# Keys turned by rows in layer 0, and exponents packed without holes in layer 1

## The chip, the cores and the metric

The kernel runs on one core of a Trainium2 chip. The metric is the device time of one execution in microseconds (us). The engines are TensorE (PE), VectorE (DVE), ScalarE (ACT), GpSimd (POOL) and SyncE (SP), which here only issues DMAs. Each engine works off its own list of instructions in order; semaphores make one wait for another.

## The reference

The reference is a decoder trunk of two layers for one sequence of 1024 tokens and width 1024, in float32. Layer 0 is gated linear attention, layer 1 sparse attention; after each mixer come a residual sum with LayerNorm and a gated per-layer embedding.

```
# layer 0: four heads, key width 256, value width 512
q_t = q * dk**-0.5 * exp(G);  k_t = k * exp(-G);  k_s = k * exp(G_last - G)
A = where(tril, q_t @ k_t.T, 0);  o = A @ v + q_t @ S
S = S * decay + k_s.T @ v                     # state, chunk after chunk
o = o * rsqrt(mean(o*o) + eps) * gn_g;  y = (o * silu(z)) @ w_out
# layer 1: sixteen heads of width 128, one shared k and v
idx = top 256 of the indexer's scores of each query
o = softmax(q @ k[idx].T * scale) @ v[idx];  y = (o * silu(z)) @ w_out
```

## The kernel before

The work is cut into two halves of 512 tokens, and both layers run half by half: layer 0 of half 0, layer 0 of half 1, layer 1 of half 0, layer 1 of half 1. An operand of a float32 matmul is split into a high and a low part in the rounded type fp32r (ACT makes the high part, DVE the low one by a subtraction); a product is then three matmuls, high by high, high by low and low by high. All projections are such matmuls of 128x512 into PSUM tiles named `pb` or `U`. Their weights (`wst`) come from DRAM and are split into `whi` and `wlo` in half 0; the parts are stored as `whs` and `wls`, and half 1 loads them from there.

The program is written in one stream by Python. A `Flow` object keeps an estimated clock of PE and a heap of steps with due times: `after(dt, f)` makes a step due dt after now, `req` puts a step back until its inputs have been emitted, `ripe(t)` until the estimated clock has reached t. The order on every engine is thus fixed when the program is built, by estimates; on the chip only semaphores wait.

**Layer 0, one head of one half.** `v_phase` makes the values of four chunks of 128 tokens, each in a loop over four 128-wide parts (t) and the two halves of the weights (kk). `qk_phase` makes the queries and keys; DVE writes the scaled keys as `m` (`ev_k`). Then four chunks go through `s1` to `s4`. `s1` computes A transposed into `tr` and, where a state follows, turns the chunk's keys with two matmuls against `ident`; `kh` and `kl` are their high and low parts. `s2` updates the state through `U`, the next step forms o, and `s4` passes on: for most heads o is turned in squares of 32 by DVE and through DRAM (`od`, `uf`), for the last head's later chunks by four transposes on PE (`oT`). The result, gated, is `u`, the operand of the output matmuls. `R` holds the states, `sc0` is scratch.

**Layer 1, `attend`.** Half 1 sees 512 past keys and its own 512; half 0 only its own. For each head and each block t of 128 queries, PE computes scores `S`; DVE adds the mask and takes the minimum (`P`, `mx`, L1592); ACT writes the exponents to `sq` with their sum (L1599). `sq` holds for each t all key blocks j up to its own; blocks above the diagonal are holes that stay zero. DVE turns `sq` in squares of 32 (L1605). SP stores it (`sqd`, L1618), four DMAs for each group i of 512 keys, and loads it back turned as `PT` (L1628), one DMA for each group. ACT and DVE split `PT` into `ph` (L1645) and the low part, which stays in `PT` (L1643), and PE multiplies with the values `vT` into `o` (three matmuls for each key block). `sq` is one tile, so a head's exponents wait until the stores of the head before have landed. The loop over heads runs in slots: while head h is multiplied with the values, the scores of head h + 1 are made, and two or three units of projections (L329, `slots`) fill PE. In half 1 slots 0 to 3 have two units, from slot 4 on three.

The lines with names such as L58 (a matmul) and L411 (a low part) are helpers.

Of the kernel before, what the change touches and what calls it, by code (L numbers as in the profile page):

```python
# [23 lines left out]
HT = 512  # L24
NK = 8
GH = 4
# [251 lines left out]
def trunk_kernel(ctx, tc, x_tok, x_T, p_T, pos, freq, g_q, g_k, g_v, g_z, g_a, g_a2, g_ba, g_gn, g_o,  # L278
# [329 lines left out]
    def qk_phase(u, X):  # L608
# [4 lines left out]
        def ev_q(d):  # L613
# [9 lines left out]
            return f  # L623

        def ev_k(d):
            def f(ps):
                dve.tensor_mul(u["k"][:, d], ps, u["k"][:, d])
            return f

# [16 lines left out]
    def core_steps(u):  # L646
# [31 lines left out]
        def s1(c):  # L678
            def f():
                cs = slice(c * 128, c * 128 + 128)  # L680
                if c == 0 and half:
                    make_S(0)
                tr = pp.tile([128, 4, 128], F32, tag="tr", name="tr")
                for d in range(2):
                    mm(tr[:, 0], k[:, d, cs], q[:, d, cs], d == 0, d == 1)
                if makes_state(c):
                    for d in range(2):
                        fl.transpose(tr[:, 1 + d], k[:, d, cs], ident)
                Af = Afs[c % 2]
                Ah = lp.tile([128, 128], F32R, tag="Ah", name="Ah", bufs=2)  # L690
# [4 lines left out]
                def a():  # L695
                    dve.copy_predicated(Af, cmask, tr[:, 0])
                    if makes_state(c):
                        act.activation(kh, tr[:, 1:3], AF.Copy)

                def b():  # L700
                    if makes_state(c):
                        lo_part(kl, tr[:, 1:3], kh)
                        st["kt", c] = kh, kl
# [97 lines left out]
        def s4(c):  # L801
            def f():
# [752 lines left out]
    def attend(st, h, half, ap, sq):  # L1555
# [7 lines left out]
        G, nb = len(groups), half + 1  # L1563
        by_key = sq.rearrange("p (b j t r) -> p t j b r", b=4, t=4, r=32)
        squares = sq.rearrange("p (b j t r) -> p t b j r", b=4, t=4, r=32)

# [4 lines left out]
        def A(t):  # L1571
            def f():
# [9 lines left out]
                if t == 0:  # L1582
                    st["sm", h] = cp.tile([128, 4], F32, tag=("ss", "rs")[h % 2], name="sm", bufs=2)
                    st["mx", h] = cp.tile([128, 3, 8], F32, tag="mid", name="mx", bufs=2)
                sm, mx = st["sm", h], st["mx", h][:, 0, t:t + 1]
                lim = 3.0e38
# [9 lines left out]
                def exp():  # L1596
                    fl.req(st["x"] == nb * h)
                    to, rows = by_key[:, t, :n // 128], P.rearrange("p (j b r) -> p j b r", b=4, r=32)
                    act.activation(to, rows, AF.Exp, scale=-1.0, bias=mx, accum_out=sm[:, t:t + 1])  # L1599
                    st["P", h, t] = True  # L1600
                    after(0.4 + n / 1000.0, turned)

                def turned():
                    x = squares[:, t, :, :n // 128]
                    dve.transpose(x, x)  # L1605
                    st["D", h, t] = True
# [3 lines left out]
        def store(i):  # L1610

            def f():
                get(*(("D", h, t) for t in range(4)))
                fl.req(st["x"] == nb * h + i)
                dt = st["dram", h, i] = dp.tile([4, 32, 4, HT], F32, tag=f"sq{i}", name="sqd", bufs=2)
                sq4 = sq.rearrange("p (b i c) -> p i b c", b=4, i=nb)
                for a in range(4):
                    nc.sync.dma_start(dt[:, :, a].rearrange("b p c -> p b c"), sq4[32 * a:32 * a + 32, i])  # L1618
                st["x"] += 1
            return f  # L1620

        def load(i):

            def f():
                dt, _ = get(("dram", h, i), ("dram", h, nb - 1))
                fl.req(st["pv"] >= (h * G - (0 if i else G - 4) if half else (h - 1) * G))
                PT = ap.tile([128, 4, HT], F32R, tag=f"PT{i}", name="PT", bufs=2 - half)
                nc.sync.dma_start(PT.bitcast(F32), dt.rearrange("b p a c -> (b p) a c"))  # L1628
# [3 lines left out]
        def parts(g):  # L1632
            def f():
# [3 lines left out]
                st["sp"] += 1  # L1637
                lo = PT.rearrange("p a (j c) -> p j a c", c=128)[:, j % 4, :, 32 * t0:]
                ph = ap.tile([128, HT], F32R, tag="ph", name="ph", bufs=3)
                hi = ph[:, :HT - 128 * t0].rearrange("p (a c) -> p a c", a=4)  # L1640

                def second():
# [7 lines left out]
        def inverse():  # L1650
            get(("P", h, 3))
            fl.req(st["x"] > nb * h)
            row = st["row", h] = dp.tile([4, 128], F32, tag="row", name="row", bufs=2)
            if in_turn:
                dve.reciprocal(st["sm", h], st["sm", h])
# [30 lines left out]
        def pv(g):  # L1686
            first, last = g == 0, g == len(groups) - 1

            def f():
# [8 lines left out]
                if last:  # L1698
                    PT, = get(("PT", h, half))
                    whole = PT.bitcast(F32).rearrange("p a (j c) -> p j a c", c=128)[:, 3, :, 96:]  # L1700
                    mm(o3[:, :, 96:], vT[0][:, base + 3].bitcast(F32), whole, False, False)
                for i, (l, r) in enumerate(((vT[0], ph), (vT[1], ph), (vT[0], pl))):
                    mm(o3[:, :, 32 * t0:], l[:, j], r, first and i == 0, last and i == 2)
                if g == len(groups) - 2:
# [3 lines left out]
                if last:  # L1708
# [10 lines left out]
                    def done():  # L1719
# [96 lines left out]
    for half in range(NH):  # L1816
# [6 lines left out]
        fl.run(*(unit(u) for u in first_units))  # L1823
        sq = ap.tile([128, (4 * half + 4) * HT], F32, name="sq")
        pool.memset(sq, 0.0)
        st["x"] = st["sp"] = st["pv"] = st["out"] = 0
# [3 lines left out]
        for h, units in enumerate(plan, -1):  # L1830
# [5 lines left out]
            if h >= 0:  # L1836
# [16 lines left out]
            if h < 15:  # L1853
# [117 lines left out]
```

## Time and profile before

| | us |
|---|---|
| median of three runs | 1934.23 (1932.59 to 1935.04) |
| the profiled execution | 1935.94 |
| its span | 1934.2 |
| PE busy | 1914.7 (99%) |
| DVE busy | 1495.4 (77%) |
| ACT busy | 1002.4 (52%) |
| POOL busy | 153.0 (8%) |

The profile is one execution; the span runs from the first instruction to the last. PE's busy time counts overlapping ends of pipelined matmuls, so the time between starts tells what a matmul costs. Hardware DMA queues were busy for 72.1% of sixteen engines' span. In the timeline a row gives start, duration, engine, line, operation, output and inputs, shapes, and in brackets how long the engine had been idle and who ended it. `SPq` is SP issuing a DMA; its time is that of the issue, not of the transfer.

### The profile page before, as it was taken

Reading aid. Unit: us, or ns where it says so; the run is one execution under the profiler, and the core shown is the slowest. Engines: PE = TensorE matmul, PEld = TensorE weight load, DVE = VectorE, ACT = ScalarE, POOL = GpSimd, SP = SyncE. Lnnn points to the kernel's source line nnn. Section 1 sums busy time; section 2 is a strip of 40 time slices with the busy share of each in tenths; the row PEclk is TensorE's granted clock in tenths of the full one; section 3 lists DMA queues with packets and bytes.
Section 4 is the critical chain, followed back from the end, with each engine's and each line's share of the span. In section 5 each row is a group of like instructions: output and inputs, shape, how many; then the busy total and the mean of one; then the engine's idle time right before and its main releaser. Section 6 shows DMA issues by size and latency. Waiting matters only on the chain.

```text
span 1934.2 us, 26875 instructions
## 1 busy us (share of the span) xinstructions
PE 1914.7 (99%) x8826; PEld 1590.6 (82%) x8826; DVE 1495.4 (77%) x3081; ACT 1002.4 (52%) x1896; POOL 153.0 (8%) x301
## 2 busy tenths in 40 slices
PE   9999999999999999999999999999999999999999
PEld 7888888888888888888888888888888778888887
DVE  5777666696778888878858987778798887777873
ACT  5564636445564646464535676756443443434432
POOL 0000000010010101010101001221001010000000
PEclk9999999999999999999999999999999999999999
DMA  4567766768667767677688588987877898888874
GB/s 156 207 218 230 225 220 215 225 207 274 223 221 262 244 224 247 222 242 228 211 287 302 169 294 288 318 293 283 305 247 283 324 305 302 299 303 289 290 285 142
DMA packets 200764, 488.91 MB, mean 253 GB/s; under 512 B 26504, under 2 KB 42928, under 8 KB 194480
## 3 DMA queue, kind: packets, MB, share of 16 engines
q1 hardware_dynamic: 193200, 474.55, 72.1%
q0 software_dynamic: 7424, 12.64, 2.0%
q8 instruction: 69, 1.13, 0.2%
q14 instruction: 71, 0.58, 0.1%
HBM read 343.18 MB, written 143.92 MB: 252 GB/s over the span
## 4 chain that ended last, share of the span: by engine, by line
PE 88%; DVE 5%; ACT 3%; DMA 2%; issue 1%; SPq 0%; DVEq 0%; ACTq 0%
PE pb L58 67%; PE o L58 8%; PE U L58 6%; PE S L58 5%; DMA PT<-sqd 1%; PE tr L58 1%; DVE sq L1605 1%; DVE PT L1643 0%; DMA wst<-in_g_v 0%; DVE sc L1141 0%; PE xt L62 0%; DVE wlo L191 0%; PE ix L58 0%; SPq L1618 0%; PE S L62 0%
## 5 line engine op out<-in xcount | busy, mean ns | idle before, releaser
L58 PE MATMUL pb<-x,whi 128*128 128x512 f32 x2272 | 704.2, 391 | 0.8 <-DVE x L411 0.7
L58 PEld LDWEIGHTS pb<-x,whi 128*128 128x128 f32 x2272 | 419.5, 188 | 80.0 <-DVE x L411 1.9
L58 PE MATMUL pb<-x,wlo 128*128 128x512 f32 x1136 | 442.6, 390 | 0.0
L58 PE MATMUL pb<-whi,u 128*128 128x512 f32 x1024 | 339.5, 392 | 1.5 <-ACT u L419 0.8
L58 PEld LDWEIGHTS pb<-x,wlo 128*128 128x128 f32 x1136 | 213.2, 188 | 45.8 <-DVE wlo L191 0.4
L58 PEld LDWEIGHTS pb<-whi,u 128*128 128x128 f32 x1024 | 192.2, 188 | 41.3 <-ACT u L419 1.2
L58 PE MATMUL pb<-wlo,u 128*128 128x512 f32 x512 | 199.6, 390 | 0.0
L191 DVE TENSOR_TENSOR wlo<-wst,whi 128x512 fp32r<-128x512 f32 x232 | 154.5, 683 | 35.1 <-ACT whi L189 34.9
L189 ACT ACTIVATE whi<-wst 128x512 fp32r<-128x512 f32 x232 | 136.4, 622 | 73.9 <-DMA wst<-in_g_k 28.8
L1599 ACT ACTIVATE sq<-P,mx 128x128 f32<-128x128 f32 (+7 forms) x128 | 98.8, 772 | 87.6 <-DVE mx L1592 58.0
L58 PE MATMUL S<-kT,q 128*128 128x512 f32 (+2 forms) x576 | 123.6, 343 | 1.7 <-DVE q L411 1.2
L1645 ACT ACTIVATE ph<-PT 128x512 fp32r<-128x512 f32 (+2 forms) x160 | 86.2, 558 | 63.0 <-PE o L58 43.4
L58 PEld LDWEIGHTS S<-kT,q 128*128 128x128 f32 x576 | 100.4, 188 | 20.5 <-DVE mx L1592 2.1
L58 PEld LDWEIGHTS pb<-wlo,u 128*128 128x128 f32 x512 | 96.2, 188 | 18.2
L1643 DVE TENSOR_TENSOR PT<-PT,ph 128x512 fp32r<-128x512 f32 (+2 forms) x160 | 92.6, 592 | 21.4 <-ACT ph L1645 21.2
L1207 ACT ACTIVATE tk<-sc,tki 128x768 f16<-128x768 f32 (+2 forms) x90 | 92.9, 1033 | 25.4 <-DVE tki L1216 21.6
L1605 DVE STREAM_TRANSPOSE sq<-sq 128x128 f32<-128x128 f32 (+7 forms) x128 | 97.7, 768 | 2.0 <-ACT sq L1599 2.0
L237 DVE TENSOR_TENSOR pst<-pst,phi 128x512 fp32r<-128x512 f32 x130 | 88.7, 682 | 7.4 <-ACT phi L233 7.4
L753 ACT ACTIVATE junk<-o 128x512 bf16<-128x512 f32 x32 | 19.1, 597 | 139.7 <-DVE ot L748 116.6
L58 PE MATMUL o<-ph,vT 128*128 128x512 f32 (+2 forms) x320 | 90.8, 365 | 0.0
L58 PE MATMUL pb<-whi,x 128*128 128x512 f32 x256 | 85.3, 392 | 0.0
L58 PE MATMUL U<-whi,x 128*128 128x512 f32 x256 | 84.6, 389 | 0.0
(330 smaller groups left out, 3400.4 us busy)
## 6 DMA issues: line engine op xcount, KB each, us to landing
whi<-whs SPq DMA_DIRECT2D x128, 512.0 KB, 6.1
wlo<-wls SPq DMA_DIRECT2D x128, 512.0 KB, 6.7
sqd<-sq SPq DMA_DIRECT2D x192, 256.0 KB, 4.4
PT<-sqd SPq DMA_DIRECT2D x48, 1024.0 KB, 7.7
whs<-phi SPq DMA_DIRECT2D x130, 256.0 KB, 4.1
wls<-pst SPq DMA_DIRECT2D x130, 256.0 KB, 4.1
wst<-in_g_z SPq DMA_DIRECT2D x32, 512.0 KB, 4.7
wst<-in_g_o SPq DMA_DIRECT2D x32, 512.0 KB, 5.1
```

The costliest lines, as they stand in the source:

```text
L58: self.pe.matmul(out, lhsT, rhs, start=start, stop=stop)
L189: self.nc.scalar.activation(hi[:, c], st[:, c], AF.Copy, scale=1.0 if gain is None else gain)
L191: self.nc.vector.tensor_sub(lo[:, c], st[:, c], hi[:, c].bitcast(F32))
L237: self.nc.vector.tensor_sub(st, st.bitcast(F32), hi.bitcast(F32))
L753: act.activation(junk, ps, AF.Square, accum_out=u["ss"][:, c:c + 1])
L1207: act.activation(junk()[:, :n], scs[j], AF.Sign, bias=cand[:, j:j + 1].bitcast(F32), accum_out=cnt[:, j:j + 1])
L1599: act.activation(to, rows, AF.Exp, scale=-1.0, bias=mx, accum_out=sm[:, t:t + 1])
L1605: dve.transpose(x, x)
L1643: dve.tensor_sub(lo, lo.bitcast(F32), hi.bitcast(F32))
L1645: chain((0, lambda: act.activation(hi, lo.bitcast(F32), AF.Copy)), (0.8, second))
```

## The change

1. In `v_phase` the order of the matmuls, first half of the weights before the second, holds for the first three chunks of the first head instead of the first alone.
2. In half 0 of layer 0 the keys of chunks 2 and 3 (heads 0 and 3) or 1, 2 and 3 (heads 1 and 2) are turned by DVE in squares of 32 (`kq`), written to DRAM by POOL (`kd`) in eight DMAs a head and read back by one into `R` of the next head or `sc0`. `kh` and `kl` are made from there, and those chunks issue no transposes on PE.
3. For the last head `s4` is ripe 2.6 instead of 1.1 after o.
4. In layer 1 the ten unmasked cells (t, j) of a head's own exponents are packed in 320 columns for each of four rows b instead of 512. A block's past and own exponents are written by instructions of their own, with sums that DVE adds up afterwards. The memsets of `sq` go. Stores and loads of the own group become 320 columns wide. In half 1 the own `PT` gets two buffers, and its load stands ahead of the past one's.

```
-            if c == h == 0:
+            if c < 3 and h == u["half"] == 0:
                 order.sort(key=lambda x: x[1])
...
+    def turned_k(u):
+        return () if u["half"] else (2, 3) if u["h"] in (0, 3) else (1, 2, 3)
+
+    def turn_k(u, kd, d):
+        h, cs = u["h"], turned_k(u)
+        n = 32 * len(cs)
+        kq = lp.tile([128, HT], F32, tag=f"S{'hl'[d]}0", name="kq")
+        dve.transpose(kq[:, :4 * n].rearrange("p (m c i) -> p c m i", m=4, i=32), u["k"][:, d, 128 * cs[0]:])
+
+        def out():
+            for a in range(4):
+                pool.dma_start(kd[:, :, a, d].rearrange("m r x -> r m x"),
+                               kq[32 * a:32 * a + 32, :4 * n].rearrange("p (m x) -> p m x", m=4))
+            if d:
+                after(4.0, back_k)
+
+        def back_k():
+            raw = (R[h + 1].rearrange("p d t -> p (d t)") if h < GH - 1 else sc0)[:, :8 * n]
+            pool.dma_start(raw, kd.rearrange("m r a d x -> (m r) (a d x)"))
+            u["kt"] = raw.rearrange("p (a d c i) -> p c d a i", a=4, d=2, i=32)
+        after(1.0, out)
...
+                by_rows = c in turned_k(u)
+                fl.req(not by_rows or "kt" in u)
...
-                if makes_state(c):
+                if makes_state(c) and not by_rows:
                     for d in range(2):
                         fl.transpose(tr[:, 1 + d], k[:, d, cs], ident)
...
-                fl.ripe(st["ot", c] + 1.1)
+                fl.ripe(st["ot", c] + (2.6 if h == GH - 1 else 1.1))
...
+        cells = ((0, 1, 0),), ((0, 2, 2),), ((0, 2, 4), (2, 3, 1)), ((0, 4, 6),)
...
-                    to, rows = by_key[:, t, :n // 128], P.rearrange("p (j b r) -> p j b r", b=4, r=32)
-                    act.activation(to, rows, AF.Exp, scale=-1.0, bias=mx, accum_out=sm[:, t:t + 1])
+                    rows = P.rearrange("p (j b r) -> p j b r", b=4, r=32)
+                    to = [(cell[:, c:c + e - j], rows[:, base + j:base + e], 8 if j else 0) for j, e, c in cells[t]]
+                    if half:
+                        to.append((past[:, t], rows[:, 0:base], 4))
+                    for x, r, i in to:
+                        act.activation(x, r, AF.Exp, scale=-1.0, bias=mx, accum_out=sm[:, i + t:i + t + 1])
...
                 def turned():
-                    x = squares[:, t, :, :n // 128]
-                    dve.transpose(x, x)
+                    get(*(("P", h, i) for i in range(t)))
+                    if half and t % 2:
+                        x = by_b[:, :, 0:HT].rearrange("p b (j x) -> p b j x", j=4)[..., 32 * t - 32:32 * t + 32]
+                        dve.transpose(x, x)
+                    if t > 1:
+                        x = by_b[:, :, HT * half:][:, :, 192 * (t - 2):192 + 128 * (t - 2)]
+                        dve.transpose(x, x)
...
-                                     [store(i) for i in range(nb)], [load(i) for i in range(nb)], [inverse, to_all])]
+                                     [store(i) for i in range(nb)], [load(i) for i in reversed(range(nb))],
+                                     [inverse, to_all])]
...
                 if half:
-                    fl.at(start + 1.5, loads[1])
...
-                    fl.at(start + (max(dur - 1.0, 18.0) if h >= 0 else 16.0), loads[0])
+                    fl.at(start + (16.5 if h >= 0 else 15.0), loads[0])
+                    fl.at(start + (max(dur - 1.0, 18.0) if h >= 0 else 16.0), loads[1])
```

PE in layer 0 of half 0, third chunk of head 0, before (`ta` and `m` are queries and keys, `x` and `whi`, `wlo` a projection):

```order
L58 MATMUL pb<-x,whi 128x512 x2
L58 MATMUL pb<-x,wlo 128x512
L58 MATMUL tr<-ta,m 128x128 x2
L62 MATMUL tr<-ident,m 128x128 x2
L58 MATMUL pb<-x,whi 128x512 x2
L58 MATMUL pb<-x,wlo 128x512
```

The same place after the change:

```order
L58 MATMUL pb<-x,whi 128x512 x2
L58 MATMUL pb<-x,wlo 128x512
L58 MATMUL tr<-ta,m 128x128 x2
L58 MATMUL pb<-x,whi 128x512 x2
L58 MATMUL pb<-x,wlo 128x512
```

The pair of transposes is gone there, and ten such pairs in all.

PE in half 0 of layer 0, last chunk of the last head, from the last matmul of o on, before:

```order
L58 MATMUL o<-S,qh 128x512
L58 MATMUL pb<-whi,u 128x512
L58 MATMUL pb<-wlo,u 128x512
L58 MATMUL pb<-whi,u 128x512 x2
L58 MATMUL pb<-wlo,u 128x512
L58 MATMUL pb<-whi,u 128x512
L62 MATMUL oT<-ident,ot 128x128 x4
```

And after the change:

```order
L58 MATMUL o<-S,qh 128x512
L58 MATMUL pb<-whi,u 128x512
L58 MATMUL pb<-wlo,u 128x512
L58 MATMUL pb<-whi,u 128x512 x2
L58 MATMUL pb<-wlo,u 128x512
L58 MATMUL pb<-whi,u 128x512 x2
L58 MATMUL pb<-wlo,u 128x512
L58 MATMUL pb<-whi,u 128x512 x2
L58 MATMUL pb<-wlo,u 128x512
L58 MATMUL pb<-whi,u 128x512 x2
L58 MATMUL pb<-wlo,u 128x512
L58 MATMUL pb<-whi,u 128x512
```

The transposes `oT` follow behind the last of these rows: fifteen output matmuls stand ahead of them instead of six.

SP in layer 1 of half 1, from the stores of head 1 to the first load of head 2, before (`whi` and `wlo` are weights of projections, `row` and `inv` the sums):

```order
L1618 DMA sqd<-sq 32x4x512 x8
L1628 DMA PT<-sqd 128x2048 x2
L1676 DMA row<-uf 4x128
L174 DMA whi<-whs 128x1024
L174 DMA wlo<-wls 128x1024
L1684 DMA inv<-row 128x512
L1618 DMA sqd<-sq 32x4x512 x8
L174 DMA whi<-whs 128x1024
L174 DMA wlo<-wls 128x1024
L1628 DMA PT<-sqd 128x2048
```

After the change, up to the loads of head 2:

```order
L1663 DMA sqd<-sq 32x4x512 x4
L1663 DMA sqd<-sq 32x4x320 x4
L1680 DMA PT<-sqd 128x1280
L1680 DMA PT<-sqd 128x2048
L1738 DMA row<-uf 4x128
L174 DMA whi<-whs 128x1024
L174 DMA wlo<-wls 128x1024
L1746 DMA inv<-row 128x512
L1663 DMA sqd<-sq 32x4x512 x4
L1663 DMA sqd<-sq 32x4x320 x4
L174 DMA whi<-whs 128x1024
L174 DMA wlo<-wls 128x1024
```

The own load (1280 columns) comes ahead of the past load (2048); behind the last row the two loads of head 2 follow in the same order, ahead of the next pair of weights.

DVE in half 1 around the first split of a head, before (`q` is a query's low part):

```order
L1605 STREAM_TRANSPOSE sq<-sq 128x4x6x32
L1643 TENSOR_TENSOR PT<-PT,ph 128x4x128
L411 TENSOR_TENSOR q<-qf,q 128x512
L1605 STREAM_TRANSPOSE sq<-sq 128x4x7x32
L1643 TENSOR_TENSOR PT<-PT,ph 128x4x128
L1605 STREAM_TRANSPOSE sq<-sq 128x32x32
L1643 TENSOR_TENSOR PT<-PT,ph 128x4x128
```

And after the change:

```order
L1647 STREAM_TRANSPOSE sq<-sq 128x4x4x64
L1700 TENSOR_TENSOR PT<-PT,ph 128x4x128
L411 TENSOR_TENSOR q<-qf,q 128x512
L1650 STREAM_TRANSPOSE sq<-sq 128x4x192
L1700 TENSOR_TENSOR PT<-PT,ph 128x4x128
L1647 STREAM_TRANSPOSE sq<-sq 128x4x4x64
L1650 STREAM_TRANSPOSE sq<-sq 128x4x128
L1562 SCALAR_TENSOR_TENSOR z<-z,pb 128x512
L1700 TENSOR_TENSOR PT<-PT,ph 128x4x128
```

Behind the first split stand three turns instead of two, two of them and a gate operation ahead of the third split.

More of the change, by code (lines that the diff above doesn't have):

```diff
@@ L623, in ev_q @@
             return f
+        kd = None if u["half"] else dp.tile([4, 32, 4, 2, 32 * len(turned_k(u))], F32, tag=f"kd{h in (0, 3)}",
+                                            name="kd", bufs=2)
         def ev_k(d):
@@ L627, in f @@
                 dve.tensor_mul(u["k"][:, d], ps, u["k"][:, d])
+                if kd is not None:
+                    after(0.9, lambda: turn_k(u, kd, d))
             return f
@@ L685, in f @@
                     mm(tr[:, 0], k[:, d, cs], q[:, d, cs], d == 0, d == 1)
-                if makes_state(c):
+                if makes_state(c) and not by_rows:
                     for d in range(2):
                         fl.transpose(tr[:, 1 + d], k[:, d, cs], ident)
+                part = lambda x: x
+                kt = tr[:, 1:3]
+                if by_rows:
+                    part = lambda x: x.rearrange("p d (a i) -> p d a i", a=4)
+                    kt = u["kt"][:, c - turned_k(u)[0]]
                 Af = Afs[c % 2]
@@ L697, in a @@
                     if makes_state(c):
-                        act.activation(kh, tr[:, 1:3], AF.Copy)
+                        act.activation(part(kh), kt, AF.Copy)
                 def b():
                     if makes_state(c):
-                        lo_part(kl, tr[:, 1:3], kh)
+                        lo_part(part(kl), kt, part(kh))
                         st["kt", c] = kh, kl
@@ L1563, in attend @@
         G, nb = len(groups), half + 1
-        by_key = sq.rearrange("p (b j t r) -> p t j b r", b=4, t=4, r=32)
-        squares = sq.rearrange("p (b j t r) -> p t b j r", b=4, t=4, r=32)
+        by_b = sq.rearrange("p (b c) -> p b c", b=4)
+        past = by_b[:, :, 0:HT].rearrange("p b (j t r) -> p t j b r", t=4, r=32) if half else None
+        cell = by_b[:, :, HT * half:].rearrange("p b (c r) -> p c b r", r=32)
+        cells = ((0, 1, 0),), ((0, 2, 2),), ((0, 2, 4), (2, 3, 1)), ((0, 4, 6),)
         def get(*keys):
@@ L1582, in f @@
                 if t == 0:
-                    st["sm", h] = cp.tile([128, 4], F32, tag=("ss", "rs")[h % 2], name="sm", bufs=2)
                     st["mx", h] = cp.tile([128, 3, 8], F32, tag="mid", name="mx", bufs=2)
+                    st["sm", h] = st["mx", h].rearrange("p a b -> p (a b)")[:, 8:]
                 sm, mx = st["sm", h], st["mx", h][:, 0, t:t + 1]
@@ L1614, in f @@
                 fl.req(st["x"] == nb * h + i)
-                dt = st["dram", h, i] = dp.tile([4, 32, 4, HT], F32, tag=f"sq{i}", name="sqd", bufs=2)
-                sq4 = sq.rearrange("p (b i c) -> p i b c", b=4, i=nb)
+                n = HT if i < half else 320
+                dt = st["dram", h, i] = dp.tile([4, 32, 4, n], F32, tag=f"sq{n}", name="sqd", bufs=2)
                 for a in range(4):
-                    nc.sync.dma_start(dt[:, :, a].rearrange("b p c -> p b c"), sq4[32 * a:32 * a + 32, i])
+                    nc.sync.dma_start(dt[:, :, a].rearrange("b p c -> p b c"),
+                                      by_b[32 * a:32 * a + 32, :, HT * i:HT * i + n])
                 st["x"] += 1
@@ L1625, in f @@
                 dt, _ = get(("dram", h, i), ("dram", h, nb - 1))
-                fl.req(st["pv"] >= (h * G - (0 if i else G - 4) if half else (h - 1) * G))
-                PT = ap.tile([128, 4, HT], F32R, tag=f"PT{i}", name="PT", bufs=2 - half)
+                fl.req(st["pv"] >= (h * G - G + 4 if i < half else (h - 1) * G))
+                if i < half:
+                    PT = ap.tile([128, 4, HT], F32R, tag="PT0", name="PT")
+                elif half:
+                    PT = ap.tile([128, 4, 320], F32R, tag="PT1", name="PT", bufs=2)
+                else:
+                    PT = ap.tile([128, 4, HT], F32R, tag="PT0", name="PT", bufs=2)
+                    PT = PT.rearrange("p a c -> p (a c)")[:, :1280].rearrange("p (a c) -> p a c", a=4)
                 nc.sync.dma_start(PT.bitcast(F32), dt.rearrange("b p a c -> (b p) a c"))
@@ L1637, in f @@
                 st["sp"] += 1
-                lo = PT.rearrange("p a (j c) -> p j a c", c=128)[:, j % 4, :, 32 * t0:]
                 ph = ap.tile([128, HT], F32R, tag="ph", name="ph", bufs=3)
                 hi = ph[:, :HT - 128 * t0].rearrange("p (a c) -> p a c", a=4)
+                if j < base:
+                    lo = PT.rearrange("p a (j c) -> p j a c", c=128)[:, j]
+                else:
+                    at, end, step = ((0, 7, 2), (3, 8, 2), (1, 9, 7))[t0]
+                    lo = PT.rearrange("p a (c r) -> p a c r", r=32)[:, :, at:end:step]
+                    hi = hi.rearrange("p a (t r) -> p a t r", r=32)
                 def second():
@@ L1653, in inverse @@
             row = st["row", h] = dp.tile([4, 128], F32, tag="row", name="row", bufs=2)
+            sm = st["sm", h]
+            if half:
+                dve.tensor_add(sm[:, 0:4], sm[:, 0:4], sm[:, 4:8])
+            dve.tensor_add(sm[:, 2:3], sm[:, 2:3], sm[:, 10:11])
+            st["sm", h] = sm[:, 0:4]
             if in_turn:
@@ L1699, in f @@
                     PT, = get(("PT", h, half))
-                    whole = PT.bitcast(F32).rearrange("p a (j c) -> p j a c", c=128)[:, 3, :, 96:]
+                    whole = PT.bitcast(F32)[:, :, 288:]
                     mm(o3[:, :, 96:], vT[0][:, base + 3].bitcast(F32), whole, False, False)
+                to = o3[:, :, 32 * t0:]
+                if j >= base:
+                    to = to.rearrange("p a (t r) -> p a t r", r=32)
                 for i, (l, r) in enumerate(((vT[0], ph), (vT[1], ph), (vT[0], pl))):
-                    mm(o3[:, :, 32 * t0:], l[:, j], r, first and i == 0, last and i == 2)
+                    mm(to, l[:, j], r, first and i == 0, last and i == 2)
                 if g == len(groups) - 2:
@@ L1823, in trunk_kernel @@
         fl.run(*(unit(u) for u in first_units))
-        sq = ap.tile([128, (4 * half + 4) * HT], F32, name="sq")
-        pool.memset(sq, 0.0)
+        sq = ap.tile([128, 4 * (HT * half + 320)], F32, name="sq")
         st["x"] = st["sp"] = st["pv"] = st["out"] = 0
```

## The prediction

> **What bounds the kernel now.** The page comes first: its first section, then the chain that ended last.
>
> ```profile
> span 1934.2 us, 26875 instructions
> PE 1914.7 (99%) x8826; PEld 1590.6 (82%) x8826; DVE 1495.4 (77%) x3081; ACT 1002.4 (52%) x1896; POOL 153.0 (8%) x301
> ...
> PE 88%; DVE 5%; ACT 3%; DMA 2%; issue 1%; SPq 0%; DVEq 0%; ACTq 0%
> ```
>
> TensorE (PE) has work for 99% of the span, and the other engines appear on the chain for about a tenth of it. Only two things can move the end: matmuls that PE no longer issues, and the 19.5 us (1934.2 − 1914.7) in which it waits. So I read next whom it waits for (columns: total us, times, longest).
>
> ```profile
> PE o L58 <- DVE PT L1643: 5.2, 6, 1.6
> ...
> PE oT L62 <- DVE ot L751: 0.8, 1, 0.8
> PE pb L58 <- ACT u L419: 0.8, 1, 0.8
> PE pb L58 <- DVE u L789: 0.7, 1, 0.7
> ```
>
> The largest item is the sparse attention of layer 1: the PV matmuls (o) wait for the low part of the turned exponents (PT). Where, the table of stretches of half 1 shows (length, then busy PE, PEld, DVE, ACT, POOL, the granted clock, the DMA engines' busy share, GB/s).
>
> ```profile
> 1490.00:1510.00 20.00, 19.85 (x94) 15.99 (x92) 17.68 (x38) 9.53 (x19) 0.00 (x0) 1.00 1.00 368
> ...
> 1530.00:1550.00 20.00, 18.81 (x85) 14.62 (x84) 17.25 (x39) 9.48 (x18) 1.97 (x4) 1.00 0.94 344
> ...
> 1590.00:1610.00 20.00, 18.25 (x87) 15.21 (x87) 16.45 (x38) 8.33 (x16) 1.97 (x4) 1.00 0.94 320
> 1490.00:1610.00 120.00, 115.93 (x539) 94.91 (x538) 102.48 (x221) 55.71 (x107) 7.95 (x16) 1.00 0.92 320
> ```
>
> Here PE is idle for 4.1 us (120 − 115.93) while the DMA engines are 92% busy. These are the slots of heads 0 to 4 in half 1, where the DMA engines bind almost as hard as PE. The clock is full, so no term of the sum comes from it.
>
> **The change, part by part.**
>
> *Keys turned through DRAM.* Twenty of the 56 transposes by matrix (tr<-ident, 128x128) go. Their price is read where a pair stands in front of other matmuls:
>
> ```profile
> 96.93 0.60 PE L58 MATMUL tr<-ta,m 128*128 128x128 f32 x4
> 97.37 0.38 PE L62 MATMUL tr<-ident,m 128*128 128x128 f32 x2
> 97.51 0.71 PE L58 MATMUL pb<-x,whi 128*128 128x512 f32 x2
> 98.05 0.40 PE L58 MATMUL pb<-x,wlo 128*128 128x512 f32 x1
> ```
>
> PE issues in a pipeline, so starts count, not durations: the four tr<-ta take 0.44 us to the next start, 0.11 each, and the transposes are of the same shape. From the first transpose to the third pb it is 0.68 us; two wide pb take 0.46 (a 128x512 matmul issues every 0.23 us), which leaves 0.22 for the pair. Twenty cost 20 x 0.111 = 2.2 us, all of it on the path, since PE waits for nothing there: **−2.2**. [...]
>
> In their place VectorE (DVE) turns eight tiles of 256 or 384 columns, POOL issues 36 DMAs, and the keys of a head return as rows. What a turn costs, two of layer 1 show:
>
> ```profile
> 1542.43 1.11 DVE L1605 STREAM_TRANSPOSE sq<-sq 128x896 f32<-128x896 f32 x1
> ...
> 1544.03 1.24 DVE L1605 STREAM_TRANSPOSE sq<-sq 128x1024 f32<-128x1024 f32 x1
> ```
>
> That is 0.13 us per 128 columns and about 0.2 beside, so some 0.6 us for 384 columns. Eight turns make at most 4.8 us of DVE, in a stage of 400 us in which only oT (below) waits for it. The question is whether the rows are back in time. The tightest case is head 1, chunk 1:
>
> ```profile
> 159.57 0.69 DVE L627 TENSOR_TENSOR m<-pb,m 128x512 f32<-128x512 f32 x1 [2.83 <-PE pb L58]
> ...
> 172.99 0.60 PE L58 MATMUL tr<-ta,m 128*128 128x128 f32 x4
> ...
> 180.48 0.62 PE L58 MATMUL U<-v,kh 128*128 128x512 f32 x2
> ```
>
> ```profile
> 547.56 2.24 POOL L1260 DMA_DIRECT2D ys<-xk  x4 [11.09 <-DVE xk L1256]
> ```
>
> ```profile
> xk<-x2s POOLq DMA_DIRECT2D x16, 256.0 KB, 6.2
> ys<-xk POOLq DMA_DIRECT2D x64, 64.0 KB, 3.3
> ...
> y<-ys POOLq DMA_DIRECT2D x16, 256.0 KB, 7.7
> ```
>
> The keys are done at 160.3. The second turn adds about 0.6, its four issues 2.2 (0.56 each), their landing 3.3, the way back 6.2 (these are medians of POOL's own transfers of like size): 172.6. ScalarE (ACT) splits them a microsecond later, and the U matmuls need them at 180.5. What waits behind POOL's last DMA, which waits for the landings, is the two small rs operations of each chunk, used only in the output stage. I cost this at nothing; 7 us of other PE work covers it, and with the cover gone it costs the lateness itself, per head.
>
> *Start.* Values of the second and third chunk now use all of the first half of the weights before the second half:
>
> ```profile
> 12.89 0.50 PE L58 MATMUL pb<-wlo,x 128*128 128x512 f32 x1 [0.62 <-DVE wlo L191]
> 14.09 0.50 PE L58 MATMUL pb<-wlo,x 128*128 128x512 f32 x1 [0.24 <-DVE wlo L191]
> ```
>
> The second wait is for the half that is now used some nine matmuls (2 us) later. It goes, the first stays: **−0.4** (0 to −0.9).
>
> *oT of the last head, later.* In half 0 fifteen pb matmuls stand ahead of the transposes instead of six:
>
> ```profile
> 402.91 0.39 PE L58 MATMUL pb<-whi,u 128*128 128x512 f32 x1
> 404.12 0.66 PE L62 MATMUL oT<-ident,ot 128*128 128x128 f32 x4 [0.83 <-DVE ot L751]
> ```
>
> From 402.91 to 404.12 is 1.21 us for an issue of 0.23: 0.98 lost. Nine more matmuls (2.0 us) cover it. What follows oT (its product with z, then the split u) is late next, by 1.1 us net, and u is needed after the output matmuls of the chunks before; a short wait there is possible, so **−0.9** (−1.0 to −0.4). In half 1 oT moves by nine matmuls too; what waited there is another tile, u at L789 (0.7), made by DVE from the squares: 0 (−0.7 to +0.5).
>
> *Own exponents without holes.* The PV matmuls keep number, widths and place. Per head of half 1 the four own stores shrink from 256 to 160 KB and the own load from 1024 to 640 KB; in half 0 likewise. What a smaller packet costs, two rows bound:
>
> ```profile
> DMA packets 12663, 38.43 MB, mean 320 GB/s; under 512 B 1872, under 2 KB 1880, under 8 KB 11117
> ...
> q1 hardware_dynamic: 12141, 38.30, 91.2%
> ```
>
> ```profile
> q1 hardware_dynamic: 193200, 474.55, 72.1%
> ```
>
> The first is the stretch 1490 to 1610, the second the whole span. Share x 16 engines x time / packets gives 144 ns at 3155 B and 115 ns at 2456 B, or 0.041 ns per byte and 14 ns fixed. An own store's packet (2048 to 1280 B, 128 in each of four stores) falls from about 98 to 67 ns: 512 x 31 / 16 = 1.0 us. The load, 384 KB less, saves another 1.0 at that rate. So 2.0 us of DMA time per head, of some 18.5 busy in a slot of 20. [...]
>
> Against that stands the order of SP's queue. Now the past load comes first and the own load stands behind; after the change it is own, then past, and own waits until its own stores have landed. Slot 3:
>
> ```profile
> 1545.33 7.48 SPq L1618 DMA_DIRECT2D sqd<-sq  x8
> 1553.12 3.29 SPq L1628 DMA_DIRECT2D PT<-sqd  x2
> ```
>
> ```profile
> 1540.55 0.63 ACT L1645 ACTIVATE ph<-PT 128x512 fp32r<-128x512 f32 x1 [3.36 <-DMA PT<-sqd]
> 1541.09 1.14 ACT L1599 ACTIVATE sq<-P,mx 128x1024 f32<-128x1024 f32 x1
> ```
>
> The two loads were issued 2.95 us apart: 3.29 less the second's own issue of 0.34. After the change past goes out about 1.9 us later (2.95 less 1.0 for the stores) and finds 640 KB ahead of it, 1.8 us at 368 GB/s. But stores and weights find emptier queues by 2.0 us a head. The second fence, of slot 2, shows why a late past load counts: the next head's last exponents stand behind the first split (ph) in ACT's queue, and the next stores behind them. There ACT issues two exponents of 512 columns instead of one of 1024, which DVE's turn in between covers. DVE turns 2304 columns in three instructions instead of 1920 in two behind the first split, 0.6 us by the turns above, ahead of the third split; the past stores go out before the last of it.
>
> So these five slots lie between −4.1 (all idle time gone) and +5 (each about 1 us later). The relief reaches every slot; the later issue is smaller where weights are queued between stores and loads, as in every second slot. So I take half of the idle time: **−2.0**. Later slots have a third unit of projection work beside the attention, which covers either.
>
> In the last slot no further head's work covers a late load:
>
> ```profile
> 1845.00 0.35 SPq L1628 DMA_DIRECT2D PT<-sqd  x1
> ...
> 1850.06 0.34 SPq L1628 DMA_DIRECT2D PT<-sqd  x1
> ```
>
> ```profile
> 1852.44 1.68 ACT L1645 ACTIVATE ph<-PT 128x512 fp32r<-128x512 f32 x3 [5.70 <-DMA PT<-sqd]
> ```
>
> ```profile
> 1854.38 0.62 PE L58 MATMUL o<-ph,vT 128*128 128x512 f32 x2
> ```
>
> Past was out at 1845.0 and split at 1852.4; PV began 1.9 us later. Own could go at 1850.1, after the change at about 1849. Past behind it lands near 1855.3, 2.9 us later than now. PE waits for 1 to 3 us less the 0.8 that it now loses on u (L419) afterwards: **+1.5** (0 to +3).
>
> Half 0 of layer 1 has slack on DMA and one exponent more per head: 0 (±1). Background splits and weight DMAs shift by a place or two: 0 (±1). The two memsets of sq leave POOL, which nobody waits for there.
>
> **Sum:** −2.2 − 0.4 − 0.9 − 2.0 + 1.5 = −4.0. The profiled execution took 1935.94, its span and 1.7 around it, and would take 1931.9; the median of the three runs is 1934.23, 1.7 lower, so the forecast on that scale is **1930.2**.
>
> **The rivals.** *A: the DMA engines alone make the waits of these five slots.* For it: 92 to 100% busy there. Then all 4.1 go, and with 0 in the last slot the sum is −7.6: 1926.6. Against it: DVE, too, is 85% busy, and PE's waits name it.
>
> *B: own ahead of past decides; slower.* If the past load lands x later in each of four slots, the loop through ACT passes it on and PE loses 4x. With −3.5 fixed and +1.5 in the last slot it decides from x = 0.5 on. With x = 1.5 (1.9 + 1.8 late, less the 2.0 of relief, rounded down) it is +4.0: 1938.2. For it: the 2.95 us and the wait for the own stores. Against it: in every second slot a pair of weights stands between the stores and the loads in SP's queue, which gives the own stores time to land before the own load comes up.
>
> *C: keys are back late.* A way back of 7.7 (y) instead of 6.2 and a busy queue would hold ACT 2 to 4 us at head 1 and 2; the 7.5 us to U hide most, S and Ah behind it do not. It would give back about 2: 1932.2.
>
> *D: the packing relieves nothing.* If a packet of 1280 B takes as long as one of 2048, the own stores keep their 1.0 us per head; the load's 1.0 is left and makes up for about half of the later issue. The five slots then give 0 and the last keeps +1.5: −2.0, 1932.2. Against it stands the fit of 0.041 ns per byte, for it that no row shows 1280 B itself. [...]
>
> **How the numbers follow.** Forecast 0.45 (of itself 1927.5 to 1932.5), A 0.19, B 0.14, C 0.09, D 0.13. A measurement of this kernel can tell about 0.2%, 3.9 us, from no change: below 1930.4 is faster, above 1938.1 slower. Faster: A and two thirds of the forecast, 0.49. Slower: the larger part of B and the upper bounds of several terms at once, 0.13. Same: the rest, 0.38. The range leaves a tenth on each side: half of A goes below 1925.5 if the start and oT give their bounds too, and half of B goes above 1938.
>
> **What would show it.** Right: 36 tr<-ident; no wait at oT in half 0 nor at 14.1; PE idle from 1485 to 1605 about 2 us; DMA share there near 0.83. Wrong: ACT waiting for keys (kh) over 2 us in half 0 of layer 0; the first ph of a head more than 17 us after its first store; a PE wait over 3 us near 1850. The forecast fails most likely by the slots' term: its two parts are each larger than their difference.

## The result, and the profile after

The changed kernel takes 1946.82 us (median of five runs, 1945.45 to 1947.86), the kernel before beside it 1935.04 (1932.59 to 1936.91): a ratio of 1.0055, 95% interval 1.0044 to 1.0067, or 8 to 13 us slower. The forecast was 1930.2, 4 us faster; the time lies above the range, on the side of rival B. The profiled execution has a span of 1946.1 us, 11.9 more than that of before.

The page of the changed kernel, its first section and the chain's shares:

```profile
span 1946.1 us, 27150 instructions
PE 1917.2 (99%) x8806; PEld 1589.6 (82%) x8806; DVE 1504.4 (77%) x3105; ACT 1027.6 (53%) x2088; POOL 166.5 (9%) x335
...
PE 17%; DVE 5%; DMA 4%; ACT 1%; issue 0%; SPq 0%; DVEq 0%; ACTq 0%
```

PE has twenty instructions fewer and is still busy for 99%; what it does not have work for grew from 19.5 to 28.9 us. The shares of the chain add up to 27%: it was followed back over the last 540 us only, where PE has less than two thirds of it. The waits of PE name the new holders (total us, times, longest):

```profile
PE o L58 <- DVE PT L1700: 12.9, 14, 1.9
PE o L58 <- ACT ph L1702: 2.1, 1, 2.1
...
PE pb L58 <- DVE u L411: 1.3, 1, 1.3
```

The first row was 5.2 us in six waits. Now both rows of PV (o) together are 15.0 us in fifteen. The stretch of half 1 that held 4.1 us of idle PE, in the same columns as in the prediction:

```profile
1490.00:1610.00 120.00, 113.94 (x524) 92.44 (x523) 101.69 (x224) 61.59 (x159) 7.95 (x16) 1.00 0.82 282
```

The DMA engines' share fell from 0.92 to 0.82, as forecast, and yet PE is idle for 6.1 us instead of 4.1. So a lighter load on the DMA engines did not by itself bring the data sooner.

Where the time went is read by comparing when the same matmul starts in each trace. The table gives the start in the kernel before and how much later (+) or earlier (−) it starts in the changed kernel and in four of the experiments below; each column is from one profiled execution.

| PE's matmul | before | changed | e1 | e2 | e4 | e3 |
|---|---|---|---|---|---|---|
| first tr of half 0 | 79.49 | −0.75 | −0.34 | −0.02 | −0.62 | −0.24 |
| first tr of half 1 | 601.91 | −3.42 | −3.10 | −2.76 | −3.65 | −2.81 |
| first PV of half 0 | 1112.14 | −3.67 | −3.19 | −2.83 | −3.18 | −3.07 |
| first PV of half 1, head 0 | 1500.39 | −1.54 | −1.04 | −2.67 | −2.90 | −1.59 |
| first PV of head 5 | 1612.37 | +1.52 | −5.27 | −3.56 | −7.09 | −3.68 |
| first PV of head 8 | 1689.82 | +1.28 | −5.45 | −3.90 | −7.24 | −3.84 |
| first PV of head 9 | 1714.81 | +4.18 | −5.02 | −3.94 | −6.79 | −3.42 |
| first PV of head 13 | 1816.86 | +7.18 | −4.34 | −3.62 | −6.16 | −2.74 |
| first PV of head 15 | 1854.38 | +9.46 | −4.30 | −3.28 | −6.12 | −2.70 |
| last matmul | 1929.87 | +11.88 | −4.46 | −2.03 | −6.25 | −2.87 |

Layer 0 gives its 3.5 us. From the first PV of half 0 to that of half 1, 2.1 are lost again; heads 0 to 4 of half 1 take 3.1, heads 8 and 12 (the steps to 9 and 13, with little between them) 5.7, and the last head, counted from the first PV of head 14 on, 4.6.

The queue of SP shows why at head 8. First the changed kernel, stores to loads, then what SP waited for in the same 18 us:

```profile
1666.59 2.68 SPq L1663 DMA_DIRECT2D sqd<-sq  x4
1669.37 1.07 SPq L174 DMA_DIRECT2D whi<-whs  x1
1670.54 1.02 SPq L174 DMA_DIRECT2D wlo<-wls  x1
1671.65 2.65 SPq L1663 DMA_DIRECT2D sqd<-sq  x4
1679.78 0.34 SPq L1680 DMA_DIRECT2D PT<-sqd  x1
1680.22 0.38 SPq L174 DMA_DIRECT2D whi<-whs  x1
1680.69 0.38 SPq L174 DMA_DIRECT2D wlo<-wls  x1
1681.16 0.38 SPq L1680 DMA_DIRECT2D PT<-sqd  x1
```

```profile
SPq L1680 <- DMA sqd<-sq: 5.3, 1, 5.3
```

In the kernel before, the same stretch reads:

```profile
1670.50 2.89 SPq L1618 DMA_DIRECT2D sqd<-sq  x4
1673.48 1.98 SPq L174 DMA_DIRECT2D whi<-whs  x1
1675.57 0.82 SPq L174 DMA_DIRECT2D wlo<-wls  x1
1676.48 0.38 SPq L1628 DMA_DIRECT2D PT<-sqd  x1
```

Before, SP went on from the last store to a pair of weights and then to the past load, whose stores had landed by then. Now the own load is next, and SP stands still for 5.3 us until the own stores, which went out last, have landed. Behind it wait the weights and the past load, the very one that PE needs first. It goes out at 1681.16, 14.6 us after the head's first store instead of 11.1, and its split and the PV matmuls follow late:

```profile
1689.17 0.63 ACT L1702 ACTIVATE ph<-PT 128x512 fp32r<-128x512 f32 x1 [2.32 <-DMA PT<-sqd]
```

```profile
1696.93 0.50 PE L58 MATMUL o<-PT,vT 128*128 128x512 f32 x1 [1.14 <-DVE PT L1700]
1700.02 0.50 PE L58 MATMUL o<-PT,vT 128*128 128x512 f32 x1 [1.42 <-DVE PT L1700]
```

In us from a head's first store, issue of the past load and first split of its data:

| head | before | changed | e1 |
|---|---|---|---|
| 1 | 10.0, 16.6 | 11.5, 18.8 | 9.5, 16.4 |
| 2 | 9.6, 18.0 | 10.1, 19.0 | 7.6, 16.4 |
| 3 | 7.8, 14.7 | 9.1, 16.6 | 6.3, 14.6 |
| 4 | 9.1, 17.8 | 9.5, 17.3 | 7.4, 16.4 |
| 8 | 11.1, 19.3 | 14.6, 22.6 | 10.1, 20.2 |
| 12 | 11.0, 18.9 | 14.3, 22.5 | 9.4, 20.2 |
| 15 | 8.2, 15.7 | 13.1, 19.1 | 7.5, 14.7 |

### The profile page after: what moved, and what is told of

The parts are those of the page before. It is cut to its first block, busy times and chain, and to the rows that moved or that the text cites. A ratio compares the mean times of both kernels' runs of the same rounds, so it can differ in the third digit from the quotient of the medians.

```text
span 1946.1 us, 27150 instructions
## 1 busy us (share of the span) xinstructions
PE 1917.2 (99%) x8806; PEld 1589.6 (82%) x8806; DVE 1504.4 (77%) x3105; ACT 1027.6 (53%) x2088; POOL 166.5 (9%) x335
## 5 line engine op out<-in xcount | busy, mean ns | idle before, releaser
L1639 ACT ACTIVATE sq<-P,mx 128x512 f32<-128x512 f32 (+2 forms) x224 | 125.5, 561 | 73.5 <-DVE mx L1628 66.6
L58 PEld LDWEIGHTS S<-kT,q 128*128 128x128 f32 x576 | 100.5, 188 | 20.2 <-DVE q L411 1.8
L787 ACT ACTIVATE junk<-o 128x512 bf16<-128x512 f32 x32 | 19.1, 597 | 144.0 <-DVE ot L782 123.3
L1726 POOL DMA_DIRECT2D row<-sums x88 | 43.9, 506 | 528.7 <-DVE sums L1722 527.9
L1628 DVE CUSTOM_DVE_ANT_0 P<-S,bias 128x512 f32<-128x512 f32 (+3 forms) x128 | 71.5, 565 | 17.5 <-PE S L58 15.3
```

What stands on the lines that cost most here:

```text
L58: self.pe.matmul(out, lhsT, rhs, start=start, stop=stop)
L787: act.activation(junk, ps, AF.Square, accum_out=u["ss"][:, c:c + 1])
L1628: dve.tensor_tensor_reduce(P[:, a:a + e], ps[:, :e], bias_t[T][:, a:a + e], op0=OP.add, op1=OP.min, scale=-ATTN_SCALE, scalar=lim, accum_o ...
L1639: act.activation(x, r, AF.Exp, scale=-1.0, bias=mx, accum_out=sm[:, i + t:i + t + 1])
L1726: pool.dma_start(row[:, 32 * a:32 * a + 32], sums[32 * a:32 * a + 4])
```

## The experiments

**The past load first again (e1_past_first).** The changed kernel with the order of the two loads put back; everything else stays.

```
-                                     [store(i) for i in range(nb)], [load(i) for i in reversed(range(nb))],
+                                     [store(i) for i in range(nb)], [load(i) for i in range(nb)],
...
                 if half:
+                    fl.at(start + 1.5, loads[1])
...
-                    fl.at(start + (16.5 if h >= 0 else 15.0), loads[0])
-                    fl.at(start + (max(dur - 1.0, 18.0) if h >= 0 else 16.0), loads[1])
+                    fl.at(start + (max(dur - 1.0, 18.0) if h >= 0 else 16.0), loads[0])
```

> The changed kernel with one thing undone: in half 1 of layer 1 the past load goes to SP's queue ahead of the own load again, at the due times of before; the own exponents stay packed and layer 0 stays changed. Theory Q (queue): the loss of half 1 comes from the own load, which stands first, waits for its own stores and holds back the past load and the weights behind it. Then the first split of head 8 comes about 19 us after the head's first store, as before (22.6 in the changed kernel), the waits at heads 9, 13 and 15 (2.9, 2.9 and 4.7 us) go, and of the 3.8 us lost from head 0 to head 4 at least half: 1936 or less, against 1946.8. Theory X (exponents): the loss comes from the split exponents and the longer turns on ACT and DVE, which stay here: 1943 or more.

1932.68 us, ratio to before 0.9981 (0.9972 to 0.9990). The whole loss is gone, and the theory of the split exponents with it, since all of these stay; the first split of head 8 comes at 20.2 us. In the table the lead no longer shrinks by more than 0.7 us from one row to the next behind head 8, and over heads 0 to 4 it grows by 4.2 us. In the stretch that had 4.1 us of idle PE, 0.6 are left:

```profile
1490.00:1610.00 120.00, 119.38 (x556) 98.87 (x556) 108.19 (x238) 64.82 (x167) 7.95 (x17) 1.00 0.85 283
```

**Layer 0 alone (e2_layer0_only).** The kernel before with points 1 to 3 of the change.

> The kernel before with the changes to layer 0 alone (order of the values' matmuls, keys turned through DRAM, oT of the last head later); layer 1 is as before. Both theories: the lead that the trace of the changed kernel shows when layer 0 ends, 3.5 us, arrives at the end: 1931 to 1932. If the lead were only made up by waits later (layer 1 bound by something other than PE), it would be 1934 to 1935.

1933.88 us, ratio 0.9987 (0.9978 to 0.9996): 2.0 us less than the 1935.88 of the kernel before run beside it, 3 to 4 expected. The lead of 2.8 us at the first PV ends as 2.0 (the last head loses 1.2 in this execution). The measurement lies between the two expectations: by the ratio's interval layer 0 gains 1 to 4 us, and the 3.5 of the one trace stand near its upper end. Scatter at the start is part of it: the first tr is 0.75 us early in that trace and 0.02 in this one, with the same instructions ahead of it.

**The own load issued by POOL (e3_own_by_pool).** The changed kernel, with one word changed for the own load of half 1.

```
-                nc.sync.dma_start(PT.bitcast(F32), ...)
+                (pool if half and i == half else nc.sync).dma_start(PT.bitcast(F32), ...)
```

> The changed kernel, but the own load of half 1 is issued by POOL instead of SP, at the same due time. It still starts ahead of the past load and moves the same 640 KB, but its wait for the own stores no longer stands in front of the past load and the weights in SP's queue. Theory Q with the wait as its cause: past loads go out as early as in the kernel before, the waits at heads 9, 13 and 15 go: 1934 to 1938. Theory Q with the data as its cause (640 KB ahead of the past load): about half of the loss stays, 1940 to 1943. Theory X: no change, 1945 to 1948.

1934.14 us, ratio 0.9991 (0.9982 to 1.0000). With the wait on another engine's queue the loss is gone. Head 8 on SP, and below it the own load on POOL:

```profile
1661.41 2.67 SPq L1663 DMA_DIRECT2D sqd<-sq  x4
...
1670.41 0.37 SPq L1680 DMA_DIRECT2D PT<-sqd  x1
```

```profile
1673.92 0.54 POOL L1680 DMA_DIRECT2D PT<-sqd  x1 [7.17 <-PE S L58]
```

The past load goes out 9.0 us after the first store. One point of the expectation was wrong: the own load goes out 3.5 us behind it, because its stores have to land first. (By the trace's semaphores the last of them landed at 1673.35; the row names PE, whose semaphore also moved just then.) So this run takes both the wait and the data out of the past load's way. For the data as a cause the traces hold nothing: from issue to split the past load of head 8 took 8.2 us before (1676.48 to 1684.66) and 8.0 with the own load ahead of it (1681.16 to 1689.17), and that of the last head 7.4 and 6.1. The issue is late, not the transfer. This is read from traces; no run has the data ahead of the past load without the wait.

**Half 0 unpacked, oT early (e4_half0_unpacked).** e1 with the exponents in 512 columns again in half 0 of layer 1 (turns, stores, loads, sums and PV operands as before), and

```
-                fl.ripe(st["ot", c] + (2.6 if h == GH - 1 else 1.1))
+                fl.ripe(st["ot", c] + 1.1)
```

> e1_past_first with two more things undone: in half 0 of layer 1 the own exponents stand in 512 columns with holes, as before (stores, loads, sums and PV operands too), and the oT transposes of the last head come at 1.1 instead of 2.6. In e1_past_first the lead over the kernel before shrinks by 2.1 us between the first PV matmul of half 0 and the first of half 1, and by 0.6 at oT. Theory S (packing costs PE in half 0: PV matmuls that read packed cells start 235 instead of 227 ns apart, and the added sums make the first inverse late): the lead stays at about 3 us through half 0 and the time is 2 to 3 us less than e1_past_first, about 1930. Rival: the loss comes from the order of background work, which the change of layer 0 shifted: the lead shrinks here too, and the time is that of e1_past_first, 1932 to 1933. oT: a wait of about 1 us comes back at oT and the one of 1.5 us on u goes, net 0.5 gained.

1931.73 us, ratio 0.9975 (0.9965 to 0.9984). The lead now holds through half 0 of layer 1 (−3.18 to −2.90, where e1 falls from −3.19 to −1.04). The steps from head to head tell how much of this is packing: from the first PV of head 0 to that of head 14 the lead shrinks by 1.6 us in each of the four traces with packed exponents in half 0 (changed, e1, e3 and e5 below), and by 0.0 in the three without (e2, e4 and e6 below). So packing does cost PE 1.6 us there. What follows, at the passage to half 1, scatters more than that: e4 loses 0.3 there, e1 0.5, e3 nothing, and e6, also unpacked, 1.9. The end comes 1.8 us earlier than in e1 by the traces, about 1 by the medians, with intervals that overlap; 2 to 3 were expected, and a new wait in half 1 of layer 0 takes half a microsecond of it. One place where the packed cells cost, two traces of the same head show, the changed kernel first and the kernel before second:

```profile
1253.65 0.62 PE L58 MATMUL o<-ph,vT 128*128 128x512 f32 x2
1254.10 0.40 PE L58 MATMUL o<-PT,vT 128*128 128x512 f32 x1
1254.34 0.39 PE L58 MATMUL pb<-whi,u 128*128 128x512 f32 x1
```

```profile
1236.37 0.39 PE L58 MATMUL o<-PT,vT 128*128 128x512 f32 x1
1236.60 0.61 PE L58 MATMUL pb<-x,whi 128*128 128x512 f32 x2
```

The matmul that reads the packed low part with a stride is followed after 0.24 us instead of 0.23. Over all of half 0 the median is 235 ns against 227, and 227 again in e4. That is 8 ns of a head that is 67 ns longer (20.17 us instead of 20.10, heads 5 to 12). Some 50 of the 67 are lost in projection matmuls, whose own operands have not changed: about a dozen of the 72 in a head take 3 to 10 ns longer; why, the traces do not show. From head 1 to head 14 the lead shrinks by 1.0 us, 0.3 of it in head 4 alone. Another 0.7 is a wait of PE for the first inverse, in head 0. One addition for the sums (L1714, 0.14 us) stands ahead of it on DVE; the rest DVE, which works without a pause there, brings along from the instructions before, and which of them are to blame was not followed up.

```profile
PE S L62 <- DVE mx L1717: 0.7, 1, 0.7
```

**The own load first for the last head alone (e5_last_own_first).** e1, with the order of the changed kernel for head 15 and no other. Slot 14 issues the loads of head 15. The edit against e1:

```
-                                     [store(i) for i in range(nb)], [load(i) for i in range(nb)],
+                                     [store(i) for i in range(nb)], [load(i) for i in (reversed(range(nb)) if h == 15 else range(nb))],
...
+                    if h < 15:
...
+                    if h == 14:
+                        fl.at(start + 16.5, loads[0])
+                        fl.at(start + max(dur - 1.0, 18.0), loads[1])
```

> e1_past_first, but for the last head of half 1 alone the own load goes ahead of the past load, as in the changed kernel. Theory Q: the past load of that head goes out about 4 us later, PE waits 2 us more at its first PV matmul and, as in the changed kernel, the granted clock falls to half for 3 us behind that wait, another 2 us: 1936 to 1938 against 1932.7, with nothing else moved. Rival: the 4.6 us that the changed kernel loses there belong to the lateness that it has gathered by then, and not to this head's own order: 1932 to 1934.

1936.13 us, ratio 0.9999 (0.9990 to 1.0008): 3.4 us more than e1, though each against its own runs of before. The profiled execution is the longest of the eleven, 1938.69. In the trace 3.6 us are lost from the first PV of head 14 to the last of head 15, 1.7 in a wait and 1.8 behind it:

```profile
1855.22 0.73 PE L58 MATMUL o<-ph,vT 128*128 128x512 f32 x2 [1.57 <-ACT ph L1702]
```

```profile
1856.00:1858.00 2.00, 2.00 (x5) 1.43 (x6) 2.00 (x4) 1.20 (x3) 0.00 (x0) 0.52 0.54 137
```

The granted clock is 0.52 there, and in the changed kernel at the same place 0.50:

```profile
1866.00:1868.00 2.00, 2.00 (x6) 1.29 (x6) 2.00 (x4) 0.94 (x2) 0.00 (x0) 0.50 0.92 336
```

So where the changed kernel loses 4.6 us (2.2 in the wait, 2.4 behind it) the last head's own order makes 3.6, without any lateness from before. This execution lost 3.7 us besides at the start of half 1, in a wait of 1.8 us for a query and a second stretch of low clock; that is not part of the edit, and the other executions profiled lose up to 1.9 there.

**oT late in half 1 only (e6_oT_by_half).** e4, with 2.6 for the last head in half 1.

> e4_half0_unpacked, but in half 1 of layer 0 the oT transposes of the last head are late again (2.6); in half 0 they stay at 1.1. In e4_half0_unpacked the trace shows, in half 1, waits of 1.2 us at oT and 1.5 on u (L823), where e1_past_first with 2.6 loses about 1.1 in all. Theory: the later oT pays in half 1 alone, so that about 0.5 us of lead stays when layer 1 begins (3.7 instead of 3.2) and the time is 0.5 less than that of e4_half0_unpacked, about 1931. Rival: what is gained at oT is lost at the next u, as in half 0, and nothing changes.

1931.02 us, ratio 0.9970 (0.9959 to 0.9981), the fastest of the kernels run and ahead of e4 by less than the intervals are wide. In the traces the term is as expected: the lead falls by 0.03 us over that place, from −2.96 to −2.93, while in e4 it falls from −3.71 to −3.18. In half 0 it is the other way round. The changed kernel has no wait at oT there, but seven microseconds later

```profile
409.38 0.73 PE L58 MATMUL pb<-whi,u 128*128 128x512 f32 x2 [1.33 <-DVE u L411]
```

which loses 1.49 us where oT had lost 0.98. An own load first without packing was not tried. At the passage to half 1 the trace of e6 loses 1.9 us where that of e4 loses 0.3, and it ends 1.8 us behind it, although the median of e6 is the lower: beyond this place one trace of each does not compare them.

## Why the prediction was wrong

**Step that failed: the later issue of the past load, set against the relief of the DMA engines.** The prediction saw the own load's wait in front of the past load and sized it at 1.9 us, from one head. The size was near: with the same packing the past load of heads 1 to 4 goes out 2.0 to 2.8 us later after the first store in the changed kernel than in e1. The relief was there too: in e1 it goes out 0.5 to 2.0 us earlier than before. What failed is the balance. The prediction let the relief outweigh the later issue and took half of the idle time as gained (−2.0). In fact the past load went out 0.4 to 1.5 us later than before in each of these heads, and heads 0 to 4 lost 3.1. e1 shows the two halves of that term apart: with the past load first the packing is worth −4.2 there, about rival A's figure; so the order alone cost 7.3.

**Later slots.** "A third unit of projection work, which covers either" failed at heads 8 and 12, predicted 0, measured 2.9 each. There a pair of weights stands between the past and the own stores, so that these land last. Just ahead of the own load SP issued nothing for 5.5 us in head 8 and 5.6 in head 12, against 1.7 to 3.7 in the heads without such a pair. The prediction took the weights between stores and loads for a help, in rival B too. They help when they follow the own stores (in heads 2 and 4, where they do, SP issued nothing for 2.0 and 1.9 us just ahead of the own load, in heads 1 and 3, with no pair there, for 3.3 and 2.6); ahead of them they delay the landing on which everything behind the own load waits. No run moves the pair; that it is the cause rests on heads 8, 12 and 15 being the only ones that have it. The order of before has it in the same heads, and I sized the term by slots 1 to 4 alone.

**Last head.** Predicted +1.5 (0 to +3), measured +4.6. The past load's data were put 2.9 us later; their split came 3.4 later after the first store (19.1 against 15.7), behind an issue 4.9 later. A pair of weights stands between the two groups of stores here too, and SP issued nothing for 5.1 us. The 2.2 us lost in the wait are what the prediction had said (1 to 3). Two other parts of the term failed. The 0.8 on u (L419), which it took off, did not go:

```profile
1876.62 0.51 PE L58 MATMUL pb<-whi,u 128*128 128x512 f32 x1 [0.74 <-ACT u L419]
```

And 2.4 us more were lost behind the wait, 1.6 of them in a stretch at half clock; the prediction had set the clock aside as full.

**Layer 0, −3.5.** The sum is right (−3.4 to −3.7 in the changed kernel) and its parts are not. The twenty transposes gave their 2.2: from the first tr of half 0 to just before the last head's the lead grows by 1.78 for sixteen of them, 0.111 each. The start gave 0.75 there, and 0.02 to 0.62 in other executions, so it cannot be told from its scatter. oT was sized at −0.9 and cost about +0.5: I had named the split u as late next, and 1.49 were lost on it. Instead a wait that the prediction had not priced shrank, that of the index matmuls at the start of layer 0's half 1:

```profile
529.35 0.73 PE L58 MATMUL ix<-v,u 128*128 128x512 f32 x2 [0.55 <-DVE v L411]
```

It was 1.7 us long; the place lost 1.86 in all and now 1.14.

**Keys through DRAM: right.** The rows were back in time; rival C did not come. In head 1, chunk 1, ACT split them at 171.94, and the U matmuls started at 178.94 without a wait. POOL wrote them in 4.7 us for a head and issued the way back when they had landed:

```profile
77.03 4.72 POOL L619 DMA_DIRECT2D kd<-kq  x8 [73.44 <-DVE kq L615]
87.87 0.58 POOL L626 DMA_DIRECT2D R<-kd  x1 [6.12 <-DMA kd<-kq]
```

**Half 0 of layer 1, predicted 0 (±1).** It cost 1.6 up to head 14, and 2.1 up to the first PV of half 1. "The PV matmuls keep number, widths and place" was true and not enough: a 128x512 matmul that reads with a stride is followed after 235 ns instead of 227, about a dozen projections a head take 3 to 10 ns longer, and the first inverse came 0.7 us late.

**Packets, rival D: wrong.** The queue's row of the changed kernel and the landing of the stores (KB, median us):

```profile
q1 hardware_dynamic: 193200, 449.39, 68.4%
```

```profile
sqd<-sq SPq DMA_DIRECT2D x128, 160.0 KB, 3.0
...
sqd<-sq SPq DMA_DIRECT2D x64, 256.0 KB, 4.0
```

By the prediction's working this is 110 ns for 2326 B, on the line of 0.041 ns per byte. The stores' medians mix the halves: the ones of 160 KB stand in both, those of 256 KB in half 1 alone, where they land in 4.2 us against 3.8 for 160 KB (1490 to 1830 us). The packets themselves decide: from 1490 to 1840 us one of 1280 B took 55 ns (median; mean 62) in the changed kernel, one of 2048 B 84 (mean 114) before: no step between the two sizes shows here.

**Rival B: right in kind.** It was given 0.14 and 1938.2. Its condition, a past load later by more than 0.5 us in several slots, was met in heads 1, 3, 8, 12 and 15 (the split comes 1.9 to 3.6 us later) and 2 (1.0), not in head 4 (0.5 earlier). Its 6.0 us for four slots were more than the 3.1 that heads 0 to 4 lost; its total was too small all the same, because it had nothing for heads 8 and 12 (5.7), for half 0 (2.1) and for the clock.

## What to carry to other kernels

SP issued its DMAs in the order of the program here, and in head 8 it stood for 5.3 us with the past load behind a load that waited; the order of the two loads cost 7.3 us over heads 0 to 4. So put a transfer that must wait for a landing behind whatever could go at once, or on a queue with nothing behind it (e3: 1934.14 us instead of 1946.82). Before a saving of bytes is credited, look which instruction issues the transfer that the bound engine waits for, and what stands ahead of it in that queue in each of the differing slots, not only in the one that is easiest to read. Packing cost PE, the bound here, 67 ns in each of heads 5 to 12 of half 0: with the wait for the first inverse, 1.6 us there took almost half of what layer 0 had gained.

## What was not expected of the hardware

In three places the granted clock fell to half for about 3.4 us: twice after a wait of PE for late data (0.52 from 1856 to 1858 us in e5, 0.50 from 1866 to 1868 us in the changed kernel), with 1.96 and 2.46 us between two starts of matmuls just before, and once at the start of half 1 in e5, after 2.18 us:

```profile
1470.00:1472.00 2.00, 2.00 (x10) 1.71 (x9) 1.37 (x5) 0.80 (x4) 0.00 (x0) 0.60 1.01 408
1472.00:1474.00 2.00, 2.00 (x7) 1.60 (x6) 0.88 (x4) 1.50 (x5) 0.00 (x0) 0.55 1.04 424
```

Gaps of 2.00 us at 1175.8 us in before and of 2.31 us at 1173.2 us in the changed kernel were followed by a full clock (1.00 up to 1178 us in both). So in these traces the gap's length alone does not decide; what does stays open. Behind the waits near 1855 and 1864 us about as much was lost again as in them: 1.8 us after 1.7 in e5, 2.4 after 2.2 in the changed kernel, 1.6 of these 2.4 at the half clock.

A strided operand (runs of 32 elements, 64 apart) made a 128x512 matmul issue every 235 ns instead of 227 (medians) in the changed kernel, in half 0 and for a head's own group in half 1.
